# Smaller mLSTM turns, a down-projection and norms without GpSimd, and the first block's scaling on VectorE, in a two-layer hybrid block

## The chip, the cores and the metric

The kernel runs on one core of a Trainium2 chip. A core has five engines, each with an instruction queue of its own that it works off in order: TensorE (PE in the profile; its weight loads are PEld), VectorE (DVE), ScalarE (ACT), GpSimd (POOL) and SyncE (SP), which here only issues DMAs. The metric is the device time of one execution in microseconds, the median of several runs; lower is better.

## The reference, cut to what matters

There are 1024 latent tokens and 256 context tokens of width 1024, and two layers. Each layer is

```
h  = modulate(rmsnorm(x, g_norm1), sh1, sc1)
pf, mq, mk, mv, mo, mg, cq, ckv, kr = split_proj(h @ w_in)
y_f = fourier_mix(pf)                                # FFT over positions and channels
y_m = mlstm_output(h_forward, h_backward, mo, g_m)   # bidirectional mLSTM, chunk by chunk
y_a = blocked_attend(queries(rmsnorm(cq)), keys(rmsnorm(ckv), kr))
x = x + ga1 * (concat(y_f, y_m, y_a) @ w_out)
x = x + ga2 * (square(relu(modulate(rmsnorm(x), sh2, sc2) @ w_up)) @ w_down)
```

`sh`, `sc` and `ga` come from `silu(c) @ w_mod + b_mod`. The context goes through the same weights in the first layer; at the end the latent stream gets one more `rmsnorm`. Where `rmsnorm` is `x * rsqrt(mean(x*x) + eps) * g`, the kernel needs the inverse root of a mean for each token.

## The kernel before, in words

Tokens lie along the free dimension in three blocks: b = 0 and b = 1 with 512 latent tokens each, b = 2 with the 256 of the context. All arithmetic is f32. A precise product is made of three fast passes (`mm3`, L131–145, whose PE lines are L134–136, L138–140 and L141–144): each operand is split into a rounded half `hi`, copied by ScalarE (L147), and a rest `lo`, one subtraction (L148) on VectorE or GpSimd, as the caller says. `csplit` does the same for the operands of the down-projection, with the engines taken in turn from a string, `DL`; `ML` names the engine for the eight splits of the first block, `KR` those of the keys' rotary part (L940–960).

The inverse root is made in `rstd_bcast` (L190–202): TensorE sums the squares over the partitions with a column of ones (L194), VectorE scales the sums (L196), `rstd_small` (L174–187) makes a first guess (L175, L176) and three Newton steps, and TensorE spreads the result over all partitions (L201); that tile is called R. The Newton steps are three VectorE operations each (L185–187), or four on GpSimd (L180–183) where the caller passes `eng`. Before the change GpSimd makes them for block 0's first norm and, by `LNE`, for the low-rank norms of queries and keys in layer 1 (L478–490).

A scheduler puts the instructions of each engine in order by priority when the program is built; `behind(...)` adds an edge that keeps an instruction behind a named one.

The stages of the program, with their stretch in the profile: the start (0 to 110 us), in which the modulation vectors are computed from streamed weights, partly by TensorE (L396) and partly by VectorE (L402, then L404), and block 0 is normalised (`load_x`, L338–359; scaled in L359, modulated in L369). The loads of blocks 1 and 2 (L342) wait for one small copy each (L340), which reads a modulation column, so that they don't run ahead of the weights. Then the input projection of layer 0 (to 345), its attention (to 724), out-projection (to 870), up-projection (to 1249), down-projection (to 1640), an edge at which layer 1's first norm begins (to 1700), and the same for layer 1: input projection to 1905, attention to 2240, out-projection to 2372, up-projection to 2650, down-projection to 2960, and the tail.

In the attention, scores go through `exp` on ScalarE (L1140) and are then multiplied with the values (PV, L1141). Between scores and PV a step calls `side_work`, which pulls the mLSTM generator forward by one piece, a turn, so many times as a quota says; when it is done, the Fourier mixer follows. The quota is the number of turns left divided by the share `RM` of the attention's steps. Turns begin with the background work (`bg`) ahead of the first head. The transposes (L834, L868) and products (L842, L912, L914) of a turn share TensorE with the attention.

The down-projection runs in four chunks of the hidden width, each with seven products of operand blocks and their sums (L1445). `put` (L1418–1427) adds a finished part to x (L1420) and in the last chunk squares it on ScalarE (L1423, L1425) and adds the square to the norm's sum (L1426), on GpSimd unless the caller names VectorE; `E0` and `E1` (from `SE`) name the engine of the last chunk's two groups. In layer 1 the end is cut by hand: `finish_(0)` scales block 0 (a copy of R to a buffer, L1481; five tiles on GpSimd, L1487; three on VectorE, L1489), while the last products of block 1 run in two halves of 256 tokens (L1576–1578), with a norm for each half and the final scaling in L1587 (GpSimd) and L1590 (VectorE).

Of the kernel before, what the change touches and what calls it, by code (L numbers as in the profile page):

```python
# [13 lines left out]
D = 1024  # L14
# [11 lines left out]
RM = (0.5, 0.8)  # L26
# [11 lines left out]
DL = "VVVG"  # L38
# [3 lines left out]
SE = ((1, 1), (1, 0))  # L42
GL = 100
TQ = 1
LNE = (0, 1)
# [9 lines left out]
KR = ((1, 0), (1, 0))  # L55
# [5 lines left out]
ML = (1, 1, 1, 1, 0, 1, 0, 1)  # L61


def build(tc, A, out, dbg=None):
# [86 lines left out]
    hk = {}  # L151
# [185 lines left out]
    def load_x(b):  # L337
        t0, n, _ = BLK[b]  # L338
        if b:
            S.copy(xT[b][:, :, 0:1], modT[0][:, 0, XJ[b - 1]:XJ[b - 1] + 1].unsqueeze(1).to_broadcast([128, 8, 1]))  # L340
        for q in range(4):
            nc.sync.dma_start(xT[b][:, 2 * q:2 * q + 2], A["x"][:, 2 * q:2 * q + 2, t0:t0 + n])  # L342
        c = [ss[b], a2[:, 2560:3072]] if b == 0 else [ss[b]]
        for k in range(8):
            if k >= len(c):
                sq = T(wk, [128, 512], tag="sq")
            dst = sq if k >= len(c) else c[k]
            S.activation(dst[:, :n], xT[b][:, k], AF.Square)
            if k >= len(c):
                p = k % len(c)  # L350
                V.tensor_tensor(c[p][:, :n], c[p][:, :n], sq[:, :n], ALU.add)
        if b == 0:
            V.tensor_tensor(ss[b], ss[b], c[1], ALU.add)
        if b == 0:
            R = rstd_bcast(ss[b], n, D, wk, pst, "t", eng=G)
            Rs = T(wk, [128, 512], tag="gw")
            S.copy(Rs, R)
            for k in range(8):
                G.tensor_tensor(xT[b][:, k], xT[b][:, k], Rs, ALU.mult)  # L359
# [68 lines left out]
    for l in range(2):  # L428
# [384 lines left out]
        def mlstm(mlp_):  # L813
# [12 lines left out]
            for p in range(9):  # L826
                for d in range(2):
# [11 lines left out]
                    V.tensor_tensor(wv[:, :, :97], vc, wcol.unsqueeze(2).to_broadcast([128, 4, 97]), ALU.mult)  # L839
                    pc = T(psL, [128, 512], tag="l")  # L840
# [12 lines left out]
                    yield  # L853
            def tail(ci, hs, mo):
# [10 lines left out]
                V.scalar_tensor_tensor(mo, mo, 1.0, hf, ALU.add, ALU.mult)  # L865
                pt = T(psL, [128, 512], tag="l")
                for i in range(3):
                    PE.transpose(pt[:, i * 128:(i + 1) * 128], mo[:, i * 128:(i + 1) * 128], ident)  # L868
# [6 lines left out]
            for ci in range(10 if ctx_all else 8):  # L875
# [14 lines left out]
                for d in range(2):  # L890
# [12 lines left out]
                    if not first:  # L903
                        pi = order[d][order[d].index(ci) - 1]
                        qw = T(mlp_, [96, 4, 128], tag="qw", bufs=2)
                        V.tensor_tensor(qw, qc, Wb, ALU.mult)
                        Cp = T(mlp_, [96, 4, 97], tag="Cp", bufs=2)
                        nc.sync.dma_start(Cp, dC[d, pi].rearrange("p (h e) -> p h e", h=4))
                    po = T(psL, [128, 512], tag="l")
                    for h in range(4):  # L910
                        o = po[:, h * 97:(h + 1) * 97]
                        PE.matmul(o, tm[:, h], vc[:, h], start=True, stop=first)  # L912
# [12 lines left out]
                    if d == 1 and pend is not None:  # L925
                        tail(*pend)
                        yield
                pend = (ci, hs, mo)
            tail(*pend)
# [143 lines left out]
        mlq = Pools()  # L1073
        gm_ = mlstm(mlq("ml", side=other))
        bg = [k_rope] + [lambda b=b: k_piece(0, b) for b in (2, 0, 1)] + prepare(0, 0) + [lambda t=t: v_piece(0, t) for t in range(5)]
        p1 = tc.cur_priority - p0
        for f_ in bg:
            with tc.high_priority(offset=p1):
                pull(gm_, 1)
                f_()  # L1080
# [24 lines left out]
        nm_ = 18 + 4 * (10 if ctx_all else 8) - len(bg) + 1  # L1105
# [3 lines left out]
        for bi, (h, qb) in enumerate(blocks):  # L1109
# [26 lines left out]
            for i, kt in enumerate(kts):  # L1136
# [4 lines left out]
                PE.matmul(po[:97, :nq], Vt[kt // 2][:, kt % 2, h % 2], PT[:, :nq], start=i == 0, stop=i == len(kts) - 1)  # L1141
# [276 lines left out]
        def put(b, j, src, sq=None, eng=None):  # L1418
            xj = xT[b][:, j]
            V.scalar_tensor_tensor(xj, src, gains(b, j), xj, ALU.mult, ALU.add)  # L1420
            if sq is not None:
                if nss[b] == 0:
                    S.activation(ss[b], xj, AF.Square)  # L1423
                else:
                    S.activation(sq, xj, AF.Square)  # L1425
                    (eng or G).tensor_tensor(ss[b], ss[b], sq, ALU.add)  # L1426
# [69 lines left out]
        for c in range(NCH):  # L1496
# [62 lines left out]
            for j in range(4):  # L1559
                put(1, 4 + j, u3[j], sc[j] if lastc else None, E1)  # L1560
# [141 lines left out]
```

## Time and profile before

| what | us |
|---|---|
| median of 3 runs | 2992.75 |
| lowest and highest of them | 2984.58, 2996.01 |
| the profiled execution's own time | 2996.41 |
| its span | 2994.6 |

| engine | busy us | instructions |
|---|---|---|
| PE | 2827.2 | 14320 |
| VectorE | 2174.0 | 4329 |
| ScalarE | 1179.8 | 2283 |
| GpSimd | 301.9 | 358 |

The mean granted clock of TensorE in the profiled execution is 0.963 of full speed. A row of the timeline gives the start and the length of a group of neighbouring instructions of one kind, and in brackets how long the engine stood idle before it and which instruction of which engine ended that. A row of the waits gives the waiting line, the line it waited for, the sum of the idle time, how often, and the longest. Busy time of PE holds waits inside its pipeline, so a PE that is busy all the time is not one at its peak.

### The profile page before, as it was taken

What the parts mean: (1) busy time and instruction counts of PE and PEld (TensorE: products, weight loads), DVE (VectorE), ACT (ScalarE), POOL (GpSimd) and SP (SyncE); (2) the same over time, 40 slices, a digit from 0 to 9 for tenths busy, and PEclk for the clock granted to TensorE, in tenths of its full rate; (3) what the DMA queues carried; (4) which work ended last, traced back from release to release, by engine and by line L of the source; (5) the groups of instructions that cost most, each with busy time, mean ns of one, the idle gap of its engine ahead of it and who ended that gap; (6) DMA issues with size and microseconds to landing.
All of it is one profiled execution on the core that took longest, in us unless ns stands there. A gap on an engine that the chain in (4) does not pass through costs nothing.

```text
span 2994.6 us, 40430 instructions
## 1 busy us (share of the span) xinstructions
PE 2827.2 (94%) x14320; PEld 2335.4 (78%) x14320; DVE 2174.0 (73%) x4329; ACT 1179.8 (39%) x2283; POOL 301.9 (10%) x358
## 2 busy tenths in 40 slices
PE   7998999999989999999999999899999999989996
PEld 6887877767878888788887888777767788868885
DVE  7779668753598888786787537368645976678887
ACT  3322245443353333243245433245433544334444
POOL 3000100000000000021124020100000000023334
PEclk7999999999999999999999999899999999999998
DMA  6424576334355554633121213455143443353321
GB/s 238 150 70 135 146 169 159 102 103 129 106 179 166 165 172 169 239 113 116 46 91 54 94 41 91 127 145 143 63 144 117 152 134 109 110 199 103 101 79 57
DMA packets 277870, 376.43 MB, mean 126 GB/s; under 512 B 63396, under 2 KB 154468, under 8 KB 276004
## 3 DMA queue, kind: packets, MB, share of 16 engines
q1 hardware_dynamic: 274788, 366.51, 39.1%
q0 software_dynamic: 576, 4.20, 0.4%
q10 hardware_dynamic: 2304, 3.15, 0.3%
q8 instruction: 113, 1.85, 0.3%
q14 instruction: 89, 0.73, 0.1%
HBM read 283.74 MB, written 90.02 MB: 125 GB/s over the span
## 4 chain that ended last, share of the span: by engine, by line
PE 67%; DVE 14%; DMA 9%; issue 6%; POOL 2%; ACT 2%; SPq 0%; DVEq 0%; POOLq 0%; ACTq 0%
PE mm L138 11%; PE mm L143 9%; PE mm L144 9%; PE v L1141 4%; PE mm L135 4%; PE mm L136 4%; PE mm L134 4%; DVE junk L235 2%; PE mm L140 2%; PE mm L141 2%; PE mm L1466 2%; DMA wf<-in_w_mt 2%; PE t L1466 2%; DVE A L148 2%; POOL A L148 1%
## 5 line engine op out<-in xcount | busy, mean ns | idle before, releaser
L138 PE MATMUL mm<-A,wr 128*128 128x512 f32 (+1 forms) x840 | 316.6, 379 | 19.9 <-DVE x L1420 6.9
L135 PE MATMUL mm<-A 128*128 128x512 f32 (+1 forms) x654 | 251.3, 389 | 12.6 <-DVE A L148 10.1
L134 PE MATMUL mm<-A 128*128 128x512 f32 (+1 forms) x654 | 238.0, 387 | 5.6 <-ACT A L147 4.4
L136 PE MATMUL mm<-A 128*128 128x512 f32 (+1 forms) x654 | 242.6, 386 | 0.3 <-DVE A L148 0.3
L143 PE MATMUL mm<-A,wr 128*128 128x512 f32 (+1 forms) x520 | 196.7, 379 | 5.0 <-DVE A L148 3.2
L138 PEld LDWEIGHTS mm<-A,wr 128*128 128x128 f32 x840 | 163.1, 195 | 49.0 <-ACT x L1192 7.3
L144 PE MATMUL mm<-A,wr 128*128 128x512 f32 (+1 forms) x520 | 195.1, 376 | 0.0
L138 PE MATMUL mm<-A,c 128*128 128x512 f32 (+1 forms) x520 | 184.7, 356 | 6.5 <-ACT A L147 5.4
L143 PE MATMUL mm<-A,c 128*128 128x512 f32 (+1 forms) x520 | 184.7, 355 | 1.6 <-DVE A L148 1.6
L144 PE MATMUL mm<-A,c 128*128 128x512 f32 (+1 forms) x520 | 183.6, 354 | 0.0
L1141 PE MATMUL v<-PT,Vt 128*97 128x512 f32 (+1 forms) x336 | 170.5, 591 | 11.3 <-ACT PT L1140 10.6
L147 ACT ACTIVATE A<-wr 128x512 fp32r<-128x512 f32 x188 | 114.3, 625 | 148.3 <-PE mm L135 59.2
L147 ACT ACTIVATE A<-A 128x512 fp32r<-128x512 f32 x174 | 106.9, 625 | 160.8 <-PE mm L135 87.2
L148 DVE TENSOR_TENSOR A<-wr,A 128x512 fp32r<-128x512 f32 x146 | 126.1, 875 | 41.6 <-ACT A L147 28.4
L135 PEld LDWEIGHTS mm<-A 128*128 128x128 f32 x654 | 123.6, 189 | 41.3 <-DVE A L148 13.6
L235 DVE SCALAR_TENSOR_TENSOR junk<-wf,t 128x512 bf16<-128x512 f32 x192 | 130.9, 682 | 33.0 <-DMA wf<-in_w_mt 31.4
L1140 ACT ACTIVATE PT<-s 128x512 f32<-128x512 f32 (+1 forms) x168 | 97.0, 583 | 129.0 <-PE s L144 128.5
L134 PEld LDWEIGHTS mm<-A 128*128 128x128 f32 x654 | 122.8, 189 | 31.1 <-ACT A L147 6.9
L136 PEld LDWEIGHTS mm<-A 128*128 128x128 f32 x654 | 123.4, 189 | 24.8 <-DVE A L148 0.7
L148 DVE TENSOR_TENSOR A<-A,A 128x512 fp32r<-128x512 f32 x131 | 116.0, 894 | 23.5 <-ACT A L147 22.6
L138 PE MATMUL mm<-wr,A 128*128 128x256 f32 x464 | 132.4, 286 | 0.5 <-ACT ev L507 0.5
L143 PE MATMUL mm<-wr,A 128*128 128x256 f32 x464 | 132.2, 286 | 0.0
(496 smaller groups left out, 7644.9 us busy)
## 6 DMA issues: line engine op xcount, KB each, us to landing
wf<-in_w_mt SPq DMA_DIRECT2D x96, 256.0 KB
x<-in_w_up SPq DMA_DIRECT2D x40, 512.0 KB
r<-in_w_up SPq DMA_DIRECT2D x38, 512.0 KB
wr<-in_w_dn SPq DMA_DIRECT2D x36, 512.0 KB
gt<-in_w_mt SPq DMA_DIRECT2D x64, 256.0 KB
da<-wf SPq DMA_DIRECT2D x64, 256.0 KB
da<-p SPq DMA_DIRECT2D x64, 256.0 KB
wf<-in_w_in SPq DMA_DIRECT2D x56, 256.0 KB
```

The costliest lines, as they stand in the source:

```text
L134: PE.matmul(ps, lh, rh, start=first, stop=False, skip_group_check=True)
L135: PE.matmul(ps, lh, rl, start=False, stop=False, skip_group_check=True)
L136: PE.matmul(ps, ll, rh, start=False, stop=last, skip_group_check=True)
L138: PE.matmul(ps, lh, rh, start=first, stop=False)
L143: PE.matmul(ps, lh, rl, start=False, stop=False)
L144: PE.matmul(ps, ll, rh, start=False, stop=last)
L147: (hi or S).activation(dst[0], src, AF.Copy) if (hi is None or hi is S) else hi.tensor_copy(dst[0], src)
L148: (lo or G).tensor_tensor(dst[1], src, f32(dst[0]), ALU.subtract)
L235: V.scalar_tensor_tensor(junk, f, 1.0, cb[w], ALU.mult, ALU.mult, accum_out=(ga, modT[l])[kh][:, w, j:j + 1])
L1140: S.activation(PT[:, :nq], ps[:, :nq], AF.Exp, scale=scale)
L1141: PE.matmul(po[:97, :nq], Vt[kt // 2][:, kt % 2, h % 2], PT[:, :nq], start=i == 0, stop=i == len(kts) - 1)
L1466: PE.matmul(o, blk[f"B{h + 1}{q + 1}"][k][:, 128 * jj:128 * jj + 128], f[:, k, 256 * h:256 * h + 256], start=h + k == 0, stop=h * k == 3)
```

## The change

GpSimd loses its part in the splits of the down-projection (`DL`), in those of block 0 (`ML`) and of the keys (`KR`), in the sums of squares of `put`, in the Newton steps (`LNE`, and `eng=G` in `load_x`) and in block 0's first scaling; VectorE takes all of it. GpSimd keeps the final scaling and small fills. The square buffers of the last group of layer 1's down-projection become four that nothing else uses there (`psl[12 + j]` in place of `sc[j]`). The mLSTM generator gives control back more often: behind the weighted values in its first phase, ahead of the output product in its second, and ahead of the transposes in `tail`; the quota counts 61 turns in place of 36 in layer 0 and 47 in place of 28 in layer 1. In layer 0 the share of the steps over which they are spread goes from 0.5 to 0.75, and the background work draws two turns for each piece in place of one. The first product of a turn's output and the transposes of `tail` are put behind the last PV that was issued.

```diff
-RM = (0.5, 0.8)
+RM = (0.75, 0.8)
-DL = "VVVG"
+DL = "V"
-SE = ((1, 1), (1, 0))
+SE = ((1, 1), (1, 1))
-LNE = (0, 1)
+LNE = (0, 0)
-KR = ((1, 0), (1, 0))
+KR = ((1,), (1,))
-ML = (1, 1, 1, 1, 0, 1, 0, 1)
+ML = (1, 1, 1, 1, 1, 1, 1, 1)
...
-            R = rstd_bcast(ss[b], n, D, wk, pst, "t", eng=G)
+            R = rstd_bcast(ss[b], n, D, wk, pst, "t")
             Rs = T(wk, [128, 512], tag="gw")
             S.copy(Rs, R)
             for k in range(8):
-                G.tensor_tensor(xT[b][:, k], xT[b][:, k], Rs, ALU.mult)
+                V.tensor_tensor(xT[b][:, k], xT[b][:, k], Rs, ALU.mult)
...
                     V.tensor_tensor(wv[:, :, :97], vc, wcol.unsqueeze(2).to_broadcast([128, 4, 97]), ALU.mult)
+                    yield
                     pc = T(psL, [128, 512], tag="l")
...
+            def after_pv():
+                return behind("pv" if hk.get("pv") else None)
...
+                yield
                 pt = T(psL, [128, 512], tag="l")
                 for i in range(3):
-                    PE.transpose(pt[:, i * 128:(i + 1) * 128], mo[:, i * 128:(i + 1) * 128], ident)
+                    with after_pv():
+                        PE.transpose(pt[:, i * 128:(i + 1) * 128], mo[:, i * 128:(i + 1) * 128], ident)
...
+                    yield
                     po = T(psL, [128, 512], tag="l")
                     for h in range(4):
                         o = po[:, h * 97:(h + 1) * 97]
-                        PE.matmul(o, tm[:, h], vc[:, h], start=True, stop=first)
+                        with after_pv():
+                            PE.matmul(o, tm[:, h], vc[:, h], start=True, stop=first)
...
-                pull(gm_, 1)
+                pull(gm_, 2)
...
-        nm_ = 18 + 4 * (10 if ctx_all else 8) - len(bg) + 1
+        nm_ = 36 + 7 * (10 if ctx_all else 8) - 2 * len(bg) + 1
...
-                PE.matmul(po[:97, :nq], Vt[kt // 2][:, kt % 2, h % 2], PT[:, :nq], start=i == 0, stop=i == len(kts) - 1)
+                hk["pv"] = PE.matmul(po[:97, :nq], Vt[kt // 2][:, kt % 2, h % 2], PT[:, :nq], start=i == 0, stop=i == len(kts) - 1)
...
-                    (eng or G).tensor_tensor(ss[b], ss[b], sq, ALU.add)
+                    V.tensor_tensor(ss[b], ss[b], sq, ALU.add)
...
-                put(1, 4 + j, u3[j], sc[j] if lastc else None, E1)
+                put(1, 4 + j, u3[j], (psl[12 + j] if last else sc[j]) if lastc else None, E1)
```

The scheduler's order moves with it. VectorE's queue at the start, before, up to the row (L404) that completes the column for which block 1's load waits; `x_39` is block 0, `A_35` its splits, `wr` are weights, and the reductions of the modulation write `mod_6`:

```order
41 L369 TENSOR_SCALAR x_39_115<-x_39_115,G_8_68,mod_6_66 128x512
42 L258 SCALAR_TENSOR_TENSOR G_8_68<-mod_6_66,vec_62 128x2 x2
43 L148 TENSOR_TENSOR A_35_105<-x_39_115,A_35_105 128x512
44 L148 TENSOR_TENSOR wr_1232<-wf_1230,wr_1232 128x512
45 L369 TENSOR_SCALAR x_39_115<-x_39_115,G_8_68,mod_6_66 128x512
46 L148 TENSOR_TENSOR A_35_105<-x_39_115,A_35_105 128x512
47 L402 SCALAR_TENSOR_TENSOR A_52_139,mod_6_66<-A_53_140,A_52_139 128x1024
48 L369 TENSOR_SCALAR x_39_115<-x_39_115,G_8_68,mod_6_66 128x512
49 L148 TENSOR_TENSOR A_35_105<-x_39_115,A_35_105 128x512
50 L402 SCALAR_TENSOR_TENSOR A_52_139,mod_6_66<-A_53_140,A_52_139 128x1024
51 L148 TENSOR_TENSOR A_35_105<-x_39_115,A_35_105 128x512
52 L404 TENSOR_SCALAR mod_6_66<-mod_6_66,vec_62 128x2
```

The same place now, from the last Newton operation (`rb_y`) on:

```order
47 L187 SCALAR_TENSOR_TENSOR rb_y_197<-rs_t_201,rb_y_197 128x4
48 L398 TENSOR_TENSOR mod_6_66<-gv_279,vec_62 128x2
49 L258 SCALAR_TENSOR_TENSOR G_8_68<-mod_6_66,vec_62 128x2 x2
50 L148 TENSOR_TENSOR wr_1224<-wf_1222,wr_1224 128x512
51 L148 TENSOR_TENSOR wr_1229<-wf_1227,wr_1229 128x512
52 L359 TENSOR_TENSOR x_39_115<-x_39_115,gw_216 128x512 x8
53 L402 SCALAR_TENSOR_TENSOR A_52_139,mod_6_66<-A_53_140,A_52_139 128x1024
54 L369 TENSOR_SCALAR x_39_115<-x_39_115,G_8_68,mod_6_66 128x512 x4
55 L398 TENSOR_TENSOR mod_6_66<-gv_332,vec_62 128x2
56 L402 SCALAR_TENSOR_TENSOR A_52_139,mod_6_66<-A_53_140,A_52_139 128x1024
57 L148 TENSOR_TENSOR A_35_105<-x_39_115,A_35_105 128x512 x4
58 L404 TENSOR_SCALAR mod_6_66<-mod_6_66,vec_62 128x2
```

All eight scalings come first, then the four modulations in a row and the four splits in a row, where before modulation and split took turns.

VectorE's queue at the last low-rank norm of layer 1, before; the Newton steps between the guess (L176) and R are on GpSimd:

```order
2299 L175 TENSOR_SCALAR rs_h_15397<-rb_v_15394 128x2
2300 L176 TENSOR_SCALAR rb_y_15396<-rb_v_15394 128x2
2301 L148 TENSOR_TENSOR wr_15557<-wf_15555,wr_15557 128x512
2302 L677 SCALAR_TENSOR_TENSOR ac_15569<-rb_15565,vec_62,ac_15569 128x510
2303 L579 SCALAR_TENSOR_TENSOR lf_15452<-lf_15452,ab_15449 104x128
```

Now the Newton steps stand in VectorE's queue, the last ten rows of which are (L677 to L679 are the mLSTM's convolution, L590 and L591 its gates):

```order
2441 L187 SCALAR_TENSOR_TENSOR rb_y_15381<-rs_t_15385,rb_y_15381 128x2
2442 L677 SCALAR_TENSOR_TENSOR ac_15551<-rb_15547,vec_62,ac_15551 128x256
2443 L677 SCALAR_TENSOR_TENSOR ac_15551<-rb_15547,vec_62,ac_15551 128x514
2444 L590 SCALAR_TENSOR_TENSOR cm_15454<-a__2543_15453 40x128
2445 L591 SCALAR_TENSOR_TENSOR cm_15454<-a__2543_15453 40x128
2446 L185 TENSOR_TENSOR rs_t_15385<-rb_y_15381 128x2
2447 L677 SCALAR_TENSOR_TENSOR ac_15551<-rb_15547,vec_62,ac_15551 128x256
2448 L186 TENSOR_TENSOR rs_t_15385<-rs_t_15385,rs_h_15382 128x2
2449 L679 SCALAR_TENSOR_TENSOR ac_15551<-rb_15547,ac_15551 128x514
2450 L187 SCALAR_TENSOR_TENSOR rb_y_15381<-rs_t_15385,rb_y_15381 128x2
```

Nine tiny operations are threaded through the other work; on PE 114 matmuls stand between this norm's sum and its R, where 64 stood.

PE's queue at the end of the program, before (`ss_3890` holds block 1's sums; `mm_24927` and `mm_25009` are its halves):

```order
12070 L135 MATMUL mm_24328<-A_3860_22698 128x256
12071 L136 MATMUL mm_24328<-A_3860_22698 128x256
12072 L194 MATMUL mm_24927<-ones_64,ss_3890_22728 128x1 x2
12073 L194 MATMUL mm_25009<-ones_64,ss_3890_22728 128x1 x2
12074 L201 MATMUL mm_24927<-cst_60,rb_y_24932 128x128 x2
12075 L201 MATMUL mm_25009<-cst_60,rb_y_25014 128x128 x2
```

And now (`t_24724` is block 0's R, which before stood 49 rows ahead of these):

```order
12068 L135 MATMUL mm_24310<-A_3860_22680 128x256
12069 L136 MATMUL mm_24310<-A_3860_22680 128x256
12070 L194 MATMUL mm_24909<-ones_64,ss_3890_22710 128x1 x2
12071 L201 MATMUL t_24724<-cst_60,rb_y_24710 128x128 x4
12072 L194 MATMUL mm_24991<-ones_64,ss_3890_22710 128x1 x2
12073 L201 MATMUL mm_24909<-cst_60,rb_y_24914 128x128 x2
12074 L201 MATMUL mm_24991<-cst_60,rb_y_24996 128x128 x2
```

Block 0's R has moved behind the last product and between the two sums of block 1.

More of the change, by code (lines that the diff above doesn't have):

```diff
@@ L925, in mlstm @@
                     if d == 1 and pend is not None:
-                        tail(*pend)
+                        yield from tail(*pend)
                         yield
                 pend = (ci, hs, mo)
-            tail(*pend)
+            yield from tail(*pend)
             yield
@@ L1073, in build @@
         mlq = Pools()
+        hk["pv"] = None
         gm_ = mlstm(mlq("ml", side=other))
```

## The prediction

> **What bounds the kernel now.** I read the page first, then PE's waits, then the busy table by stage, and last the timeline where a wait stands. From the page, the engines (busy time, share of the span, instructions) and the shares of the chain that ended last:
>
> ```profile
> PE 2827.2 (94%) x14320; PEld 2335.4 (78%) x14320; DVE 2174.0 (73%) x4329; ACT 1179.8 (39%) x2283; POOL 301.9 (10%) x358
> ...
> PE 67%; DVE 14%; DMA 9%; issue 6%; POOL 2%; ACT 2%; SPq 0%; DVEq 0%; POOLq 0%; ACTq 0%
> ```
>
> PE is idle for 2994.6 − 2827.2 = 167 us. POOL, the engine that the change empties, is 2% of the chain, some 60 us at most. What PE waits for (line, releaser, then us in all, times, longest):
>
> ```profile
> PE v L1141 <- ACT PT L1140: 10.6, 15, 2.0
> PE mm L194 <- DVE ss L1578: 10.2, 1, 10.2
> PE mm L135 <- DVE A L148: 10.1, 4, 6.3
> ...
> PE t L201 <- POOL rb_y L183: 8.3, 2, 5.0
> ...
> PE l L842 <- ACT x L147: 5.6, 1, 5.6
> ```
>
> No wait is large; each place that the change touches holds a few us. The busy table for a steady chunk of the down-projection in layer 1, one in layer 0, the two attentions, the edge behind the down-projection of layer 0 and the start of that of layer 1 (length; PE, PEld, DVE, ACT, POOL busy; granted clock, DMA share, GB/s):
>
> ```profile
> 2706.00:2783.40 77.40, 76.61 (x338) 62.91 (x337) 68.77 (x86) 36.26 (x64) 25.16 (x14) 1.00 0.33 109
> 1257.00:1361.00 104.00, 104.00 (x461) 87.28 (x460) 77.49 (x94) 36.34 (x64) 21.63 (x14) 0.99 0.29 91
> 345.00:724.00 379.00, 351.44 (x1943) 265.13 (x1943) 246.25 (x655) 162.47 (x377) 4.92 (x41) 0.97 0.49 131
> 1905.00:2240.00 335.00, 310.56 (x1635) 233.60 (x1633) 222.25 (x552) 140.75 (x305) 7.80 (x37) 0.95 0.47 127
> 1636.00:1660.00 24.00, 23.31 (x109) 18.61 (x107) 22.77 (x37) 12.76 (x24) 10.36 (x10) 1.00 0.21 88
> 2637.00:2676.00 39.00, 26.31 (x103) 20.64 (x104) 38.73 (x43) 14.43 (x26) 10.66 (x6) 0.87 0.49 184
> ```
>
> In the steady chunks PE has nothing idle and runs at full clock: there no other engine's work is worth anything. In the last row VectorE is busy for 38.7 of 39 us and PE for 26.3: there VectorE is the bound. In the attentions PE is idle for 27.6 and 24.4 us, and the clock stands at 0.97 and 0.95.
>
> **Part 1, the down-projection without GpSimd.** A chunk gives up 14 splits on POOL and VectorE takes them over. VectorE's first groups in the layer 1 chunk (busy, mean ns of one, idle before):
>
> ```profile
> L148 DVE TENSOR_TENSOR A<-A,A 128x512 fp32r<-128x512 f32 x19 | 16.1, 862 | 2.5 <-ACT A L147 2.2 <-PE mm L134 0.3
> L148 DVE TENSOR_TENSOR A<-wr,A 128x512 fp32r<-128x512 f32 x19 | 12.6, 684 | 3.7 <-PE mm L135 2.0 <-ACT A L147 1.7
> ```
>
> The same split takes 684 ns in one group and 862 ns on average in the other: some of its 19 stood beside a POOL operation. Taking 684 as the undisturbed time, over all groups of this stretch the excess is about 6.2 us, an estimate of 0.44 us for each of the 14 POOL operations. In a full queue one split follows the last after about 12.6/19 = 0.66 us or somewhat less (I take 0.61, the step between neighbouring splits in the timeline). So VectorE's load goes from 68.8 to 68.8 − 6.2 + 14 × 0.61 = 71.1 of 77.4 us. PE stays the bound with 6.3 us to spare: 0 for the six steady chunks.
>
> Where VectorE is the bound the balance counts: at the start of layer 1's down-projection (2637–2676) and at the edge of layer 0 (1636–1660). Its largest groups there, first of the one, then of the other:
>
> ```profile
> L148 DVE TENSOR_TENSOR A<-A,A 128x512 fp32r<-128x512 f32 x10 | 9.6, 975 | 0.3 <-ACT A L147 0.3
> ...
> L148 DVE TENSOR_TENSOR A<-A,A 128x512 fp32r<-128x512 f32 x4 | 6.0, 1504 | 0.0
> L148 DVE TENSOR_TENSOR A<-wr,A 128x512 fp32r<-128x512 f32 x4 | 4.8, 1223 | 0.0
> ```
>
> Over 684 ns these hold 10 × 0.29 + 4 × 0.82 + 4 × 0.54 = 8.4 us of excess, and smaller groups some 2 more, which goes; the 13 operations that POOL has in the two places (6 and 7, beside three tiny fills) come in, 13 × 0.61 = 7.9. Taken: −2. Ends: +8, if nothing of the excess goes, and −13, if POOL's whole busy time there (10.7 + 10.4) was taken from VectorE: 21 − 8.
>
> The Trainium skill, page "SBUF — State Buffer", section "SBUF: two separate sides", says that a VectorE operation with two SBUF inputs and a GpSimd operation that reads SBUF share one port pair as an exclusive lock, and that the loser blocks fully. By that rule the end of −13 would be the value. The 0.44 us found beside 25.16/14 = 1.8 us of POOL time speaks against it as an average.
>
> **Part 2, the start.** POOL's scaling, with what stands around it on VectorE, PE and the queue that loads block 1 (start, duration, and in brackets the idle time before; among them one row of PE's busy table):
>
> ```profile
> 27.02 1.28 DVE L148 TENSOR_TENSOR wr<-x,wr 128x512 fp32r<-128x512 f32 x2
> ...
> 32.35 12.04 POOL L359 TENSOR_TENSOR x<-x,gw 128x512 f32<-128x512 f32 x8 [2.83 <-ACT gw L357]
> ...
> 36.29 1.22 PE L138 MATMUL mm<-A,wr 128*128 128x512 f32 x2 [1.43 <-ACT A L147]
> ...
> 41.61 0.80 PE L143 MATMUL mm<-A,wr 128*128 128x512 f32 x1 [3.25 <-DVE A L148]
> ...
> 43.17 1.50 DVE L369 TENSOR_SCALAR x<-x,G,mod 128x512 f32<-128x512 f32 x1
> ...
> 46.34 0.54 DVE L369 TENSOR_SCALAR x<-x,G,mod 128x512 f32<-128x512 f32 x1
> ...
> 49.15 0.22 DVE L404 TENSOR_SCALAR mod<-mod,vec 128x2 f32<-128x2 f32 x1
> ...
> 49.69 7.18 SPq L342 DMA_DIRECT2D x<-in_x  x8
> ...
> 66.00:72.00 6.00, 4.08 (x26) 0.96 0.00 0
> ...
> 87.42 0.73 PE L138 MATMUL mm<-A,wr 128*128 128x512 f32 x2 [2.77 <-ACT A L277]
> ```
>
> Beside POOL's eight multiplications L369 takes 1.50 us, free of them 0.54. VectorE is full until 28.3 anyway, and the last Newton operation now stands behind a weight split: I put it at 30.4 (28.3, the split, nine steps of some 0.16), about 1 us later than POOL's last step now; so R and its copy come 1 us later too, and the scaling starts at 33.3 instead of 32.35. Then eight multiplications on VectorE at 0.61 end at 38.2 (POOL: 44.4), one reduction of 1.2, four L369 at 0.5, another reduction, four splits, and L404 at about 45.2 against 49.15. That row frees block 1's loads (49.69): 4 us earlier. Against it, PE's first product moves from 36.3 to 40.5 and its steady work from 41.6 to about 43; it has 1.9 us of idle later (66 to 72) and the 2.77 at 87.42 to make that up, so it is through with block 0 at about 84. Block 1 starts there instead of at 87.4: −3. Ends: −6 (the whole load gain plus a shorter slow clock) and +2 (only PE's delay).
>
> **Part 3, the low-rank norms of layer 1.**
>
> ```profile
> 1790.93 0.57 POOL L180 TENSOR_TENSOR rs_t<-rb_y 128x2 f32<-128x2 f32 x1 [10.56 <-DVE rb_y L176]
> ...
> 1801.42 0.71 PE L201 MATMUL t<-cst,rb_y 128*128 128x128 f32 x4 [3.31 <-POOL rb_y L183]
> ...
> 1802.30 0.63 PE L138 MATMUL mm<-A,wr 128*128 128x512 f32 x1
> ...
> 1805.85 0.40 PE L138 MATMUL mm<-A,wr 128*128 128x512 f32 x1
> ```
>
> POOL needs 10.4 us for twelve tiny operations, PE runs dry for 3.31 us and then goes on at half clock to about 1805.5 (0.63 against 0.40 a product), which costs 1.7 more. In the new order PE has 114 matmuls between the sum and the last R instead of 64, by these durations some 21 us of cover for 12, and VectorE's nine Newton operations are threaded through other work of about 17 us. So the wait goes: −5; ends −6 and 0 (VectorE's queue is held up once on the way and is late by those same 3 us).
>
> **Part 4, the attention.** Each mLSTM turn is cut in two or three, turns are drawn at 1.04 a step in layer 0 (61 over 0.75 of 78 steps; before 36 over 0.5, 0.92) and 0.84 in layer 1 (before 0.5), and transposes and first products now wait for the last PV. Smaller pieces can only win what PE lacks ahead of PV: the 10.6 us of L1141, and part of the 5.6 at L842. I counted from the order how much other PE work stands between the scores and their PV: the pairs with less than 0.9 us of it are 24 of layer 0 before and 30 after, so the stall stays. The key rope on VectorE alone spares its splits the slowing of part 1 and may shorten the one wait of 5.6 us by 1 to 2. Taken: −2. Ends: −14 (both waits gone, 10.6 + 5.6, less 2) and +8 (the waits of L1141 come a second time, less 2).
>
> **Part 5, the tail.**
>
> ```profile
> 2963.67 7.65 POOL L1487 TENSOR_TENSOR A<-x,c 128x512 f32<-128x512 f32 x5 [7.72 <-ACT c L1481]
> ...
> 2971.36 0.63 ACT L1425 ACTIVATE c<-x 128x512 f32<-128x512 f32 x1 [0.37 <-POOL A L1487]
> ...
> 2963.65 5.33 DVE L1489 SCALAR_TENSOR_TENSOR A<-x,vec,c 128x512 f32<-128x512 f32 x3 [0.64 <-ACT c L1481]
> ...
> 2976.05 2.77 DVE L1578 TENSOR_TENSOR ss<-ss,c 128x256 f32<-128x256 f32 x8 [5.50 <-POOL ss L1426]
> ...
> 2968.12 0.28 PE L136 MATMUL mm<-A 128*128 128x256 f32 x1
> 2978.63 1.84 PE L194 MATMUL mm<-ones,ss 128*128 128x1 f32 x8 [10.22 <-DVE ss L1578]
> ...
> 2986.81 1.22 PE L201 MATMUL mm<-cst,rb_y 128*128 128x128 f32 x4 [3.63 <-DVE rb_y L187]
> ...
> 2988.47 2.05 DVE L1590 SCALAR_TENSOR_TENSOR A<-x,vec,mm 128x256 f32<-128x256 f32 x5
> ```
>
> The last square waits for POOL's scaling to let go of a buffer (2971.36), POOL adds it, VectorE's sums follow at 2976: from the last product to the sum matmul 10.2 us. After the change the square has a buffer of its own and the adds follow at once, so the first sum can stand right behind the last product. But the R of block 0 now comes behind all products too, its scaling (POOL's 7.65, VectorE's 5.33) with it, and VectorE's Newton steps of block 1 stand behind that 5.33. Counted from 2968.2: copy of R at +2.0, VectorE's three operations to +7.7, nine Newton steps to +9.5, first R to +10.9, second R at +13.2 to +14.4 (now 2988.0, +19.8), the last scaling to +16.9 (now 2990.5, +22.3). −5.4; block 0's output now goes out beside block 1's, for which I take 1.4 off: −4. Ends: −8 (VectorE's 5.33 falls to 2 without contention) and +2 (the transfers end last).
>
> **Sum.** Profiled execution: 2996.41 us, span 2994.6. 0 − 2 − 3 − 5 − 2 − 4 = −16, so 2980.4. The median of the runs shown, 2992.75, stands 3.7 under that execution: 2977.
>
> **Rivals.** What a measurement of this kernel can tell from no change is about 0.5%, 15 us (bounds 2977.8 and 3007.7).
>
> Gains eaten: in the start PE's later first product cancels the earlier loads, the tail ends with its transfers, the low-rank R is late by something else. Left are 0 to −8; about 2989. For it: PE is the bound nearly everywhere, and each term is one wait whose next one I only estimated.
>
> Attention fills: smaller turns, drawn more evenly, and PV put ahead of them close PE's gaps. The two windows hold 52 us of idle and 379 × 0.03 + 335 × 0.05 = 28 of slow clock; with half of that gone, −40 in place of −2: 2977 − 38 = 2939. For it: 24 to 28 us idle in each. Against: only 10.6 of them are L1141's.
>
> Whole blocking: a POOL operation holds VectorE up for all its time, and the two edges gain 13 in place of 2: 2977 − 11 = 2966. The page on SBUF named in part 1 states it. Against it stands the 862.
>
> VectorE the bound of the down-projection, on the other side: 14 operations more in one in-order queue. If each costs more than (8.6 + 6.2)/14 = 1.06 us there, counting what waits for ACT behind it, VectorE is late in a chunk. Priced by the longest wait of PE for a split, 6.3 us, in each of six steady chunks: +38, 2977 + 38 = 3015. Against it: 0.68 for a free split, and 6.3 us of room.
>
> That the change does not do what it says is small: POOL keeps the final scaling and small fills, all else is seen to move.
>
> **How the numbers follow.** Forecast (gain of 8 to 24) 0.45; gains eaten 0.20; attention fills 0.14; whole blocking 0.06; VectorE the bound 0.15. Faster by over 0.5%: half of the first (0.24), the third and fourth: 0.44. Slower: the last and the worst of the second, 0.16. Same: 0.40. The range: the forecast's ends, −47 and +20 if all fell to one side, are unlikely together; low 2950 leaves out most of the attention case, high 3000 leaves out the last: 2950 to 3000. The forecast alone: 2969 to 2985.
>
> **What would show it.** Right: no wait of L201 on POOL; block 1's first product near 84; the second R of block 1 some 15 us behind the last product instead of 19.8; steady chunks still at 77.4 and 104 with VectorE near 71 in the first; L148 at 684 in both groups. Wrong: chunks over 78 with PE waiting on L148 (VectorE the bound), attention windows shorter by 10 or more, or the start's 87.4 kept.

## The result, and the profile after

The changed kernel took 2971.3 us (median of 5 runs, 2965.9 to 2974.0), the kernel before 2988.4 (5 runs, 2984.6 to 2996.0): a ratio of 0.9938, 95% interval 0.9923 to 0.9953. In a later set on one chip, with 5 runs of the one and 11 of the other, it was 0.9951 (0.9936 to 0.9966). So it is faster by 15 to 19 us, where 2977 and a gain of 16 were forecast. The profiled execution took 2973.98 us with a span of 2972.2, 22.4 under that of before, whose profiled execution (2996.41) was slower than its five runs.

The page after, in the parts shown of before (engines, then the shares of the chain):

```profile
PE 2818.6 (95%) x14320; PEld 2330.3 (78%) x14320; DVE 2181.7 (73%) x4535; ACT 1177.2 (40%) x2283; POOL 31.8 (1%) x134
...
PE 73%; DVE 13%; DMA 9%; issue 3%; ACT 2%; SPq 0%; POOL 0%; DVEq 0%; POOLq 0%; ACTq 0%
```

GpSimd lost 270 us of work and 224 instructions; VectorE took over 206 instructions and is busy for only 7.7 us more (2174.0 to 2181.7). That is the first sign of what happened: with GpSimd silent, VectorE's own operations became shorter by almost as much as it took over. PE's waits after (line, releaser, sum, times, longest):

```profile
PE mm L138 <- ACT A L147: 20.3, 6, 6.6
PE mm L201 <- DVE rb_y L187: 12.1, 2, 8.5
PE mm L138 <- ACT rb L673: 10.7, 5, 4.6
PE v L1150 <- ACT PT L1149: 10.0, 17, 1.7
```

All waits for R on GpSimd are gone, and the sum matmul's 10.2 us at the end with them; in the tail a wait of 8.5 us for the first half's R has taken its place. The wait for the exponential, 10.6 us before, is 10.0.

By landmarks of the timeline (for a stage, from the start of its first product to the start of its last), the 22.4 us came from these places: the R of block 1 in the start 7.8 earlier; layer 0's down-projection 433.6 us before and 428.8 after; layer 1's, up to its last 96 products, 317.7 and 311.1, and these last ones 0.8 less; the tail from the last product to the end 26.2 and 23.4. What lies between moves by a few us in both directions. Layer 0's attention, from the first PV to the last, took 326.6 and 325.5, layer 1's 264.4 and 268.0. Each of these is one execution. In the profiles of the seven kernels here with the old turns, layer 0's attention takes 321.1 to 328.6 us, and in the five with the old start block 1's R comes at 77.5 to 80.7 (in the nine with the new one at 72.0 to 74.5). So a few us in one stage of one profile can be chance.

In the start, VectorE's scaling and the row that frees block 1's loads; then PE's first products of block 0 and of block 1, in the profile of the changed kernel (start, length, idle time before):

```profile
32.45 4.91 DVE L359 TENSOR_TENSOR x<-x,gw 128x512 f32<-128x512 f32 x8 [0.90 <-ACT gw L357]
...
43.87 0.22 DVE L404 TENSOR_SCALAR mod<-mod,vec 128x2 f32<-128x2 f32 x1
```

```profile
39.68 1.22 PE L138 MATMUL mm<-A,wr 128*128 128x512 f32 x2 [2.91 <-ACT A L147]
...
80.35 1.22 PE L138 MATMUL mm<-A,wr 128*128 128x512 f32 x2 [2.59 <-ACT A L277]
```

Eight scalings take 4.9 us where GpSimd needed 12.0. L404 is 5.3 us earlier than before; PE begins 3.4 us later, and block 1 begins 7.1 us earlier all the same.

A steady chunk of layer 1's down-projection after (length; PE, PEld, VectorE, ACT, GpSimd; clock, DMA), and below it its largest groups on VectorE:

```profile
2737.40:2814.10 76.70, 76.47 (x338) 62.91 (x337) 71.06 (x102) 35.92 (x64) 0.00 (x0) 1.00 0.33 110
```

```profile
L148 DVE TENSOR_TENSOR A<-wr,A 128x512 fp32r<-128x512 f32 x28 | 18.4, 686 | 2.6 <-ACT A L147 2.6
L148 DVE TENSOR_TENSOR A<-A,A 128x512 fp32r<-128x512 f32 x21 | 14.0, 688 | 2.4 <-ACT A L147 2.4
```

And all that PE waited for in the same chunk before:

```profile
PE mm L135 <- POOL A L148: 0.8, 1, 0.8
```

VectorE's load was forecast at 71.1 and is 71.06, the splits shown take 686 and 688 ns, and the chunk is 0.7 us shorter than before (77.4): PE's one wait in it was for a split on GpSimd.

### The profile page after: what moved, and what is told of

Same layout as the page of the kernel before. It is cut to its first block, busy times and chain, and to the rows that moved or that the text cites. A ratio compares the mean times of both kernels' runs of the same rounds, so it can differ in the third digit from the quotient of the medians.

```text
span 2972.2 us, 40262 instructions
## 1 busy us (share of the span) xinstructions
PE 2818.6 (95%) x14320; PEld 2330.3 (78%) x14320; DVE 2181.7 (73%) x4535; ACT 1177.2 (40%) x2283; POOL 31.8 (1%) x134
## 4 chain that ended last, share of the span: by engine, by line
PE 73%; DVE 13%; DMA 9%; issue 3%; ACT 2%; SPq 0%; POOL 0%; DVEq 0%; POOLq 0%; ACTq 0%
PE mm L138 12%; PE mm L143 10%; PE mm L144 10%; PE mm L135 5%; PE mm L134 5%; PE mm L136 5%; PE v L1150 4%; PE mm L140 2%; PE mm L141 2%; PE mm L1475 2%; PE t L1475 2%; DVE junk L235 1%; DVE A L148 1%; DVE ac L677 1%; PE t L134 1%
## 5 line engine op out<-in xcount | busy, mean ns | idle before, releaser
L138 PE MATMUL mm<-A,wr 128*128 128x512 f32 (+1 forms) x840 | 314.5, 377 | 26.4 <-ACT A L147 14.8
L135 PE MATMUL mm<-A 128*128 128x512 f32 (+1 forms) x654 | 249.8, 386 | 5.9 <-DVE A L148 5.9
L136 PE MATMUL mm<-A 128*128 128x512 f32 (+1 forms) x654 | 247.5, 386 | 0.0
L134 PE MATMUL mm<-A 128*128 128x512 f32 (+1 forms) x654 | 227.0, 387 | 7.4 <-ACT A L147 7.4
L143 PE MATMUL mm<-A,wr 128*128 128x512 f32 (+1 forms) x520 | 193.5, 372 | 0.2 <-DVE A L278 0.2
L144 PE MATMUL mm<-A,wr 128*128 128x512 f32 (+1 forms) x520 | 193.0, 371 | 0.0
```

Of the source, the lines that this page charges most:

```text
L134: PE.matmul(ps, lh, rh, start=first, stop=False, skip_group_check=True)
L135: PE.matmul(ps, lh, rl, start=False, stop=False, skip_group_check=True)
L136: PE.matmul(ps, ll, rh, start=False, stop=last, skip_group_check=True)
L138: PE.matmul(ps, lh, rh, start=first, stop=False)
L143: PE.matmul(ps, lh, rl, start=False, stop=False)
L144: PE.matmul(ps, ll, rh, start=False, stop=last)
```

## The experiments

The theory after the result: the time comes from places where VectorE works beside GpSimd, or PE waits for a GpSimd operation, and the turns bring nothing. The first rival: the turns make the gain. The second, of the down-projection: VectorE is full there. All ratios below are to the kernel before on the same chip (median of that set 2983 to 2985 us), so that 0.1% is 3.0 us.

**One part at a time.** Four kernels, each the kernel before with one part of the change. The first has only block 0's part:

```diff
-ML = (1, 1, 1, 1, 0, 1, 0, 1)
+ML = (1, 1, 1, 1, 1, 1, 1, 1)
-            R = rstd_bcast(ss[b], n, D, wk, pst, "t", eng=G)
+            R = rstd_bcast(ss[b], n, D, wk, pst, "t")
-                G.tensor_tensor(xT[b][:, k], xT[b][:, k], Rs, ALU.mult)
+                V.tensor_tensor(xT[b][:, k], xT[b][:, k], Rs, ALU.mult)
```

> The kernel before with only block 0's scaling, its first norm's Newton steps and its splits on VectorE. Theory (the gain lies where VectorE is freed from what runs beside it on GpSimd: start, starts of chunks, tail): 7 to 9 us less, all of it up to block 1's first product, which comes near 80 instead of 87.4. Rival (turns, or the whole order, make the gain): within 3 us of before, because PE's later first product takes the earlier loads back.

Measured: 0.9974 (0.9960 to 0.9987), 7.8 us less. As the theory has it; the rival's 3 us lies outside the interval (3.9 to 11.9). In its profile block 1's first product comes at 79.4 (87.4 before).

The second has the down-projection's part:

```diff
-DL = "VVVG"
+DL = "V"
-SE = ((1, 1), (1, 0))
+SE = ((1, 1), (1, 1))
-                    (eng or G).tensor_tensor(ss[b], ss[b], sq, ALU.add)
+                    V.tensor_tensor(ss[b], ss[b], sq, ALU.add)
-                put(1, 4 + j, u3[j], sc[j] if lastc else None, E1)
+                put(1, 4 + j, u3[j], (psl[12 + j] if last else sc[j]) if lastc else None, E1)
```

> The kernel before with only the down-projection's splits and sums of squares on VectorE and the last group's own square buffers. Theory: 12 to 16 us less, some 4 to 5 in layer 0's down-projection and edge, 7 in layer 1's, 3 in the tail; PE's waits of 0.78 us at the starts of layer 1's chunks go. Rival (VectorE is full there): 0 to 3 us less, tail only. Rival (whole blocking): over 18 less.

Measured: 0.9965 (0.9952 to 0.9979), 10.4 us less with ends of 6.3 and 14.3. In its profile layer 1's down-projection takes 311.1 us up to the last 96 products and the tail 23.4, both as in the whole change, and layer 0's 427.9. Both rivals' figures lie outside; the middle is a little under the theory's 12, which lies inside.

The third has only the low-rank norms:

```diff
-LNE = (0, 1)
+LNE = (0, 0)
```

> The kernel before with only layer 1's low-rank norms' Newton steps on VectorE. Theory: 2 to 4 us less, the wait of 3.31 us of the last R gone, part of it given back later in the same stage. Rival (order decides): no change, 0 plus or minus 2.

Measured: 1.0003 (0.9988 to 1.0018), from 3.6 us less to 5.4 more. That is no change, as the rival has it, but by the time alone the theory's 2 us is not excluded. PE's waits between the low-rank norms and the attention of layer 1, beside the 5.6 us of L842 that the prediction shows; first before, then in this kernel:

```profile
PE m L1003 <- DVE mx L1004: 3.3, 2, 2.2
PE l L842 <- DVE Mb L839: 2.3, 1, 2.3
```

```profile
PE l L842 <- DVE Mb L839: 7.4, 2, 5.3
PE mm L138 <- ACT rb L673: 2.7, 2, 2.1
PE m L1003 <- DVE mx L1004: 2.5, 2, 2.0
```

The 3.31 us of the last R are gone, but that R drew other products ahead of it, and a new wait of 2.7 us for the convolution's input (L673) stands a little later; the changed kernel has the same one there, with 3.3 us. The gain was given back inside the same stage: from the end of layer 0's down-projection to the first PV of layer 1, the nine profiles with these Newton steps on VectorE take 298.3 us on average, and the five with them on GpSimd 298.3 too.

The fourth has only the turns:

```diff
-RM = (0.5, 0.8)
+RM = (0.75, 0.8)
...
+                    yield
...
+                    with after_pv():
+                        PE.transpose(pt[:, i * 128:(i + 1) * 128], mo[:, i * 128:(i + 1) * 128], ident)
...
+        nm_ = 36 + 7 * (10 if ctx_all else 8) - 2 * len(bg) + 1
```

> The kernel before with only the smaller turns, their order behind PV and the new quota; GpSimd keeps all its work. Theory: the turns bring nothing, 0 to 5 us more, layer 0's attention some 1 shorter and layer 1's 3 to 4 longer. Rival (turns make the gain): 8 us less or better.

Measured: 1.0013 (0.9999 to 1.0027), 3.9 us more, not clear of nothing. The rival falls. Layer 0's attention took 329.3 us and layer 1's 265.3 (before 326.6 and 264.4); the 1 us forecast for layer 0 is too small to be seen in one profile.

**All but the turns.** The changed kernel with the old turns, quota and order:

> The changed kernel without the turns: all of GpSimd's work on VectorE, the turns, their quota and their order as before. Theory (parts add, the turns cost 2 to 4): 18 to 22 us under the kernel before, some 3 under the changed one. Rival (turns and freed VectorE need each other): 12 us under before or less, over the changed kernel.

Measured: 0.9940 (0.9926 to 0.9953), 18 us less. The parts add up (0.26% + 0.35% less 0.03% is 0.58%, each with an end of 0.13 to 0.15), and the whole gain is there without the turns. The keys' splits (`KR`), which this kernel has too, were not run alone. That it beats the changed kernel, 0.9938 and 0.9951 in two sets, is not shown.

**GpSimd's work back, its results not used.** The changed kernel, in which GpSimd repeats one of four splits into a spare buffer:

```diff
+        def again(src, c):
+            if (nc_[0] + nc_[1]) % 4 == 3:
+                G.tensor_tensor(psl[-1], src, f32(c[:, 0]), ALU.subtract)
+            return c
...
-            return csplit(src, DL, cA[nc_[0] % len(cA)])
+            return again(src, csplit(src, DL, cA[nc_[0] % len(cA)]))
```

(and the same for the other operand)

> The changed kernel, in which GpSimd makes one of four splits of the down-projection's operands a second time into a buffer that nobody reads; VectorE still makes all that are used, so the output is the same and no engine waits for GpSimd's result. Theory (GpSimd's operations slow VectorE's): 6 to 12 us over the changed kernel, VectorE's splits up to 0.86 us on average again, and PE's waits at the starts of layer 1's chunks back or longer than before. Rival (what cost time was that PE waited for a split of 1.5 to 2 us on GpSimd itself): within 3 us of the changed kernel.

Measured: 1.0092 (1.0077 to 1.0107), 27.5 us over the kernel before and 42 to 46 over the changed one. The theory had the direction and was too low by a factor of about four, the rival falls. A steady chunk of it, and then its groups on VectorE:

```profile
2756.20:2838.80 82.60, 77.86 (x337) 62.84 (x336) 77.56 (x101) 35.91 (x64) 36.00 (x14) 1.00 0.32 102
```

```profile
L148 DVE TENSOR_TENSOR A<-wr,A 128x512 fp32r<-128x512 f32 x28 | 18.6, 696 | 1.7 <-ACT A L147 1.7
L148 DVE TENSOR_TENSOR A<-A,A 128x512 fp32r<-128x512 f32 x20 | 16.2, 831 | 1.0 <-ACT A L147 1.0
...
L1459 DVE TENSOR_TENSOR A<-wr,A 128x1024 f32<-128x1024 f32 x4 | 5.9, 1486 | 0.0
```

Fourteen GpSimd operations that nobody waits for make VectorE busy for 6.5 us more (71.06 to 77.56), 0.46 us each; the forecast's estimate was 0.44. VectorE has the whole load and the slowing now, and the chunk is 5.9 us longer. In it PE waited for VectorE, and VectorE for GpSimd:

```profile
PE mm L135 <- DVE A L148: 3.5, 3, 1.4
PE mm L134 <- DVE x L1434: 1.2, 3, 0.9
```

```profile
DVE wr L1459 <- POOL p L1413: 1.2, 1, 1.2
DVE r L1459 <- POOL p L1413: 1.2, 1, 1.2
```

PE's waits for VectorE are 4.7 us, where the changed kernel's chunk has 0.2. VectorE stands idle for 2.4 us because a buffer that it is to write is still being read by GpSimd, and that part is of this experiment's own making. In layer 0's chunks, where VectorE is busy for 76 of 104 us, the same fourteen operations make a chunk only 1.1 us longer (103.8 to 104.9). So this is, in kind, the forecast's rival of a VectorE that becomes the bound: 71 us of 76.7 leave room, 77.6 and 2.4 of waiting do not. How the 5.9 us divide between the two was not separated.

**The tail.** In the changed kernel VectorE's three scalings of block 0 stand ahead of the Newton steps of block 1. Here they are held until behind them:

```diff
-                    V.scalar_tensor_tensor(o, xT[b][:, k], g_, sc[1], ALU.mult, ALU.mult)
+                    held.append((o, xT[b][:, k], g_, out[:, k, 512 * b:512 * b + 512]))
+                    continue
...
+                for o, x_, g_, to in held:
+                    with behind("rs"):
+                        V.scalar_tensor_tensor(o, x_, g_, sc[1], ALU.mult, ALU.mult)
+                    nc.sync.dma_start(to, o)
```

> The changed kernel, in which VectorE's three scalings of block 0 at the end stand behind the Newton steps of block 1's second half. Theory (in the changed kernel those three operations hold up the first half's Newton steps, PE's wait of 8.46 us): 2 to 4 us under the changed kernel, the wait for the first R 4 us or less. Rival (the transfers or GpSimd's scaling end last): no change.

Measured: 0.9948 (0.9934 to 0.9961), no change from the changed kernel. These ratios can't tell 2 us from nothing, but the profile can: its tail takes 24.9 us, the changed kernel's 23.4. The tail of the changed kernel on VectorE and PE:

```profile
2950.63 0.16 DVE L186 TENSOR_TENSOR rs_t<-rs_t,rs_h 128x2 f32<-128x2 f32 x1
2950.85 5.19 DVE L1498 SCALAR_TENSOR_TENSOR A<-x,vec,c 128x512 f32<-128x512 f32 x3
...
2964.15 3.85 DVE L1599 SCALAR_TENSOR_TENSOR A<-x,vec,mm 128x256 f32<-128x256 f32 x9
```

```profile
2948.57 0.28 PE L136 MATMUL mm<-A 128*128 128x256 f32 x1
...
2959.43 1.22 PE L201 MATMUL mm<-cst,rb_y 128*128 128x128 f32 x4 [8.46 <-DVE rb_y L187]
2964.29 1.22 PE L201 MATMUL mm<-cst,rb_y 128*128 128x128 f32 x4 [3.64 <-DVE rb_y L187]
```

And with the scalings held back, on VectorE, GpSimd and PE:

```profile
2945.84 1.09 DVE L185 TENSOR_TENSOR rs_t<-rb_y 128x2 f32<-128x2 f32 x1
2946.96 1.19 DVE L186 TENSOR_TENSOR rs_t<-rs_t,rs_h 128x2 f32<-128x2 f32 x1
2948.19 1.19 DVE L187 SCALAR_TENSOR_TENSOR rb_y<-rs_t,rb_y 128x2 f32<-128x2 f32 x1
```

```profile
2945.66 6.14 POOL L1496 TENSOR_TENSOR A<-x,c 128x512 f32<-128x512 f32 x5 [824.09 <-ACT c L1490]
```

```profile
2952.06 1.22 PE L201 MATMUL mm<-cst,rb_y 128*128 128x128 f32 x4 [6.34 <-DVE rb_y L187]
```

The tiny Newton operations, 0.16 us alone, now take 1.1 to 1.2 each beside GpSimd's scaling, one for each of its operations (6.14/5 = 1.23). The wait for the first R is 6.34 us and not the 4 that the theory had. The first R comes 2 us sooner after the last product, and the end does not, because block 0's three tiles are written later and the transfers run to the end. The rival holds.

The buffer alone, on the kernel before:

```diff
-                put(1, 4 + j, u3[j], sc[j] if lastc else None, E1)
+                put(1, 4 + j, u3[j], (psl[12 + j] if last else sc[j]) if lastc else None, E1)
```

> The kernel before with only the last group's own square buffers in layer 1's down-projection; GpSimd still adds the squares. Theory (in the tail the shared buffer is a good part of the wait): the first square no longer waits for GpSimd's scaling, but the additions stand behind that scaling in GpSimd's queue, so 0 to 1 us less. Rival (the buffer alone is the tail's gain): 3 us less.

Measured: 0.9985 (0.9974 to 0.9996), 4.5 us less with ends of 1.2 and 7.8. In its profile the order of the end changed: from the first of the last 96 products to the last it takes 18.5 us (12.7 before), from there to the end 18.5 (26.2), together 2.0 less. The whole change has 3.7 less there (0.8 and 2.9), so the buffer alone, in an order of its own, brings about half of it: more than the theory's 0 to 1, less than the rival's 3.

Block 0's R ahead of the last products again, in the changed kernel and in the one without the turns:

```diff
                     finish_(0, lastc)
+                    hk["R0"] = hk["R"]
...
+                        with behind("R0" if th == 0 and k == 3 else None):
+                            mm3(X[j][:, tl], bs_[k][:, 0, sl], bs_[k][:, 1, sl], as_[k][:, 0, tl], as_[k][:, 1, tl], False, k == 3, part=True)
```

> The changed kernel, in which block 1's last products of the first half (the fourth operand) stand behind block 0's R on PE, so that R, block 0's scaling and its transfers come some 60 products before the end instead of behind them. Theory (the tail of the changed kernel is a queue of block 0's work, first on VectorE beside GpSimd, then in the transfers): 4 to 8 us under the changed kernel, 15 to 19 us from the last product to the end instead of 23.3. Rival (block 0's scaling only moves the wait ahead of the last products): no change.

> The same on the kernel without the turns (all of GpSimd's work moved, turns as before). Theory: the same 4 to 8 us under the run without the turns, 23 to 27 us under the kernel before. Rival: 18 us under before, as without it.

Measured: 0.9962 (0.9947 to 0.9977) with the turns, 0.9947 (0.9931 to 0.9964) without; neither is better than the kernel that it was made from. From the last product to the end it takes 15.5 us in both, as expected, but the last 96 products take 19.3 instead of 11.9. PE and the busy table of that stretch in the first of them:

```profile
2944.90 1.87 PE L201 MATMUL t<-cst,rb_y 128*128 128x128 f32 x8 [1.91 <-DVE rb_y L187]
```

```profile
2941.00:2948.00 7.00, 5.09 (x32) 4.89 (x31) 3.97 (x15) 3.09 (x7) 0.52 (x1) 0.80 0.01 2
2948.00:2958.00 10.00, 7.29 (x59) 7.09 (x57) 9.85 (x16) 2.84 (x7) 7.42 (x5) 0.97 0.57 211
```

PE waits for R, goes on at a lower clock (0.80 in the first row), and then waits 2.7 us for VectorE, which is full with block 0's scaling (9.85 of 10 us): the wait only moved ahead of the last products, as the rival has it.

**The share of the steps.** The changed kernel with the old share:

```diff
-RM = (0.75, 0.8)
+RM = (0.5, 0.8)
```

> The changed kernel with the old share of 0.5 of layer 0's steps for the turns. Theory (layer 0's attention waits for the exponential, not for other work): within 3 us of the changed kernel. Rival (the later turns fill gaps): 5 us or more over it, layer 0's attention longer.

Measured: 0.9930 (0.9916 to 0.9944), 2964.1 us; the changed kernel beside it:

> The changed kernel itself, for comparison on the same chip. Theory: 15 to 20 us under the kernel before.

Measured: 0.9951 (0.9936 to 0.9966), 2969.5 us, 14.6 less than before by the ratio. The rival falls: the share of 0.75 is no gain. The middle values are 6 us apart, more than the theory's 3, though the intervals allow 3. With 0.5 the kernel is the fastest of all that were run (2958.2 to 2964.4 in 5 runs, the changed one 2964.3 to 2972.2). Layer 0's attention took 320.9 us against 325.4, but kernels with one and the same attention differ by as much. The intervals overlap by a little, so that it beats the changed kernel is likely, not certain; that it beats the kernel before is.

## Why the prediction came out right, point by point

The total and the direction were right, the terms were not: two were too small and three too large. That they made up for each other is luck.

*The down-projection* was forecast at −2; alone it brought 10.4 with the tail, some 7.6 without the tail's 2.8. The balance on VectorE was exact (71.1 forecast, 71.06 measured, and 0.44 us a GpSimd operation against 0.46). What failed is the step "PE has nothing idle in the steady chunks": the row showed 76.61 of 77.40, and the missing 0.79 was a wait of PE for a split that GpSimd made. There are three such waits in the program, 2.3 us in all. The rest of the term came, as forecast in kind, where VectorE is the bound. At the start of layer 1's down-projection it was 3 us, where the forecast had 2 for that place and the edge of layer 0 together. VectorE is as full there as before, but it does 49 operations in the time in which it did 43:

```profile
2624.90:2663.90 39.00, 27.93 (x109) 21.75 (x110) 38.44 (x49) 14.60 (x27) 0.00 (x0) 0.87 0.52 188
```

Of layer 0's 4.8 us only half, at its edge, can be put down to the change: the other 2.4 lie between its first product and its 97th (49.9 us before, 47.5 after), and there the first experiment's profile, with the old splits, is as short (47.6). The rival of a full VectorE was right about the danger, and it took the load of the sixth experiment to bring it about. Whole blocking as an average price is refuted by the same number, 0.46 us for a GpSimd operation that lasted 36.00/14 = 2.57 us.

*The start* was forecast at −3, with an end of −6, and brought 7.8. The earlier loads were read rightly (L404 at 43.87, forecast 45.2, and the loads behind it 5 us earlier). The step that failed is that PE would be through with block 0 only at 84. PE's busy table in the start, the same two stretches before and after:

```profile
66.00:72.00 6.00, 4.08 (x26) 3.12 (x25) 5.90 (x14) 2.87 (x7) 1.29 (x1) 0.96 0.00 0
72.00:78.00 6.00, 6.00 (x33) 5.33 (x33) 4.89 (x21) 1.20 (x3) 0.00 (x0) 0.76 0.41 98
```

```profile
66.00:72.00 6.00, 6.00 (x48) 5.79 (x47) 4.18 (x19) 1.08 (x2) 0.00 (x0) 1.00 0.61 191
72.00:78.00 6.00, 5.76 (x49) 5.56 (x48) 2.13 (x9) 1.02 (x3) 0.00 (x0) 1.00 0.63 190
```

The gaps at 66 to 72 are gone and the slow clock behind them too (0.76 to 1.00): PE did 97 matmuls from 66 to 78 instead of 59 (of which 4 and 13 are of the wide form, 128x512), and was through at 77.8. The forecast had counted the idle time as slack, and in its middle value not the slow clock behind it. The gap and a slow clock behind it (0.79 and 0.82) are also in the profiles of the second and third experiments, whose start is the old one; in the first experiment's both are gone. That the gap causes the slow clock was not tested apart: in the fourth experiment's profile and in that of the buffer alone, also with the old start, the slow stretches lie elsewhere (0.72 from 54 to 60 us, 0.52 from 60 to 66, with PE busy throughout), and block 1's R comes 3 us earlier than before.

*The low-rank norms* were forecast at −5 and bring nothing (third experiment). The wait went as forecast; the step that failed is that nothing else is late next: a wait for the convolution's input took its place.

*The attention* was forecast at −2, with the waits for the exponential to stay. They stayed (10.0 us, 17 times). The turns alone are 0 to 8 us slower, and the old share is as fast or faster; so the sign of the term was most likely wrong, its size within the ends. The −2 was to come from the one wait of 5.6 us at L842; in the profile after it is 4.9 us, 0.7 less, and the smaller turns, taken as free, cost more than that. Which of the turns' pieces costs, and why layer 1's attention takes 268 to 270 us in the five profiles with the whole change, and 264 to 267 in all others, was not settled.

*The tail* was forecast at −4 and brought 2.8. The mechanism was right in the main: VectorE's three scalings (5.19 us, forecast 5.3) stand ahead of the Newton steps, and the first R comes 10.6 us after the last product (forecast 10.9). The second R came at 15.4 instead of 13.2, since its Newton steps waited for the first R and ran beside GpSimd. That is the part that was mis-sized. The transfers, for which the forecast took 1.4 off, took nothing more: from the second R to the end it is 7.8 us before and 7.9 after.

## What to carry to other kernels

A silent second engine can be worth more than a helping one: price an operation given to GpSimd by what it adds to VectorE's own operations (here 0.46 us of each) and by the longest wait for its result, not by its busy time off the chain. Where a table shows an engine at 99%, ask what the missing percent is, chunk by chunk; and where a wait of PE is taken away, look for what is late next, and see whether a slow clock behind the wait goes with it. Undo a bundle part by part before keeping it: here two parts, the start and the down-projection, made the whole gain.

## What the runs showed of the hardware

Beside GpSimd a tiny VectorE operation can wait as long as a large one: 128x2 operations of 0.16 us took 1.09 to 1.19 each while GpSimd scaled tiles of 128x512, one VectorE operation for each GpSimd operation of 1.23 us. There each did wait for a whole GpSimd operation, as the Trainium skill has it on the page "SBUF — State Buffer" (section "SBUF: two separate sides": whichever starts first gets the pair for the whole instruction).

In the chunk of the sixth experiment the average is far less, 0.46 us for a GpSimd operation of 2.57. The trace of the kernel before shows both sides of it. In the stretch from 2706 to 2900 us, 61 splits stood beside no GpSimd operation and took 0.68 us, and 41 stood beside one and took 0.89 on average, 1.80 at most; GpSimd's own operations took 1.29 us at least and 5.44 at most. So now the one engine waited and now the other, and a long GpSimd operation is in part one that waited.

VectorE's operations with an operand in PSUM (`mm`) pass it by: 741 ns before and 746 after, and 17 of the 35 in that stretch stood beside a GpSimd operation. With the same operand copied to SBUF (`c`), they took 877 ns before and 748 after (the groups in a steady chunk, before and then after):

```profile
L1420 DVE SCALAR_TENSOR_TENSOR x<-mm,mod,x 128x512 f32<-128x512 f32 x14 | 10.0, 741 | 0.0
L1420 DVE SCALAR_TENSOR_TENSOR x<-c,mod,x 128x512 f32<-128x512 f32 x8 | 6.7, 877 | 0.0
```

```profile
L1429 DVE SCALAR_TENSOR_TENSOR x<-mm,mod,x 128x512 f32<-128x512 f32 x14 | 9.9, 746 | 0.5 <-PE mm L136 0.5
L1429 DVE SCALAR_TENSOR_TENSOR x<-c,mod,x 128x512 f32<-128x512 f32 x8 | 5.6, 748 | 0.0
```

GpSimd was slowed too. A group of its splits in a chunk of the kernel before, and then one in the sixth experiment, where VectorE had more to do, 1.94 us each and 3.84:

```profile
L148 POOL TENSOR_TENSOR A<-wr,A 128x512 fp32r<-128x512 f32 x8 | 15.5, 1944 | 32.4 <-ACT A L147 32.4
```

```profile
L1413 POOL TENSOR_TENSOR p<-r,A 128x512 f32<-128x512 f32 x4 | 15.4, 3839 | 11.8 <-ACT A L147 11.8
```

The twelve tiny Newton operations on GpSimd show it most plainly. In the kernel before, an early low-rank norm of layer 1 has them beside an idle VectorE, and the last one beside a VectorE that is busy for 10.05 of 10.50 us; they keep GpSimd busy for 2.47 and for 9.54 us:

```profile
1752.60:1756.00 3.40, 3.40 (x16) 2.82 (x15) 0.00 (x0) 1.26 (x2) 2.47 (x12) 1.00 0.05 12
1790.90:1801.40 10.50, 7.22 (x43) 6.07 (x41) 10.05 (x21) 4.63 (x9) 9.54 (x12) 1.00 0.49 91
```
